# Second MLP: the first two products of units 0 to 2 moved ahead into the output projection's last token tiles

## The chip, the cores and the metric

One core of a Trainium2 chip runs the whole kernel as one launch. The metric is device time in microseconds (us) of that core; the figure to compare is the median over runs. PE is the matrix engine, VectorE (DVE in the profile), ScalarE (ACT) and GpSimd (POOL) are the elementwise engines, and SyncE (SP) issues the transfers. Each engine works through its own instructions strictly in the order in which the built program has them.

## The reference

A trunk of two layers over 1024 tokens of 1024 channels, all in fp32: layer 0 mixes by pooling, layer 1 by differential attention; each layer ends in a gated MLP with a convolution over three tokens.

```python
h = h + _diff_attention(_rms_norm(h, mix_norm[1]), ...)          # ends in o @ w_o, the output projection
h = h + _conv_ffn(_rms_norm(h, ffn_norm[1]), w_up[1], conv_w[1], conv_b[1], w_down[1])

def _conv_ffn(x, w_up, conv_w, conv_b, w_down):
    g, u = jnp.split(x @ w_up, 2, axis=-1)          # w_up is 1024 x 5632
    gc = conv_b + (three taps of g along the tokens)
    return (gelu(gc) * u) @ w_down                  # 2816 hidden channels
```

The change is about the seam between the two lines: the end of `o @ w_o` of layer 1, and the up half (`x @ w_up`) of the MLP behind it.

## The kernel before

**Up half of the MLP.** The 2816 hidden channels are 22 units of 128. For a unit, gate and up products are made together by a scheme of seven block products instead of eight: `product(j, i, acc, first)` is product i of unit j. Each is 12 matmuls of 128x512, four slices of the depth by three: fp32 operands are split in a high and a low part, and hi*hi, lo*hi and hi*lo are summed. The seven right operands `ar.x[i]` are shared by all units. `x[1]` and `x[2]` are the two depth halves of `hnT[0]`, so the normalized tokens of tiles 0 to 3 alone; `x[5]` and `x[3]` are `hnT[1]`, and `x[6]`, `x[7]`, `x[4]` are `xb` (the names x0, x1, x2 in the program): these five need tiles 4 to 7 as well. A unit's order is products 1, 6, 2, 7, 5, 4, 3. They accumulate in three PSUM tiles, `up_a` (1, 2), `up_b` (6, 7, 4) and `up_c` (5, 3).

**Weights.** `load(j)` issues two loads of 512 KB on SP into the `raw` pool (4 buffers, two units): the up half and then the gate half. `prep(j)` makes the seven left operands: four sums or differences of halves of them (`s_tile`, buffers from the `s` pool, 128x512), and for each product `parts`: ACT casts to `w_hi`, POOL subtracts to get `w_lo`, both into the `wc` pool (16 buffers, so eight products). For unit 0 VectorE does most of POOL's part. So POOL has 11 operations of 128x512 for each unit, four `s` and seven `w_lo`. When a unit's `s` and `w_lo` operations have read a `raw` buffer for the last time, SP may issue the load of the unit two further into it.

**The seam.** `wo_rest(tt)` does the output projection of one token tile, 24 matmuls `wo_acc` (L1251) from the 16 `wo_l` tiles that lie in `wc`; then residual and norm (`norm_to_x`): `xs` on ACT, eight transposes `tp` on PE (L299), and then, one tile later (`each_with_lag`), `combine` writes the operands of that tile (`put`: ACT the high part, VectorE or POOL the low part). Tiles 4 to 7 need the kept `xf` of tiles 0 to 3. The order of the tiles is `ORDER`. `next(mlp)` within it loads and prepares unit 0 early.

**What sets the order.** In the loop over units 1 to 21 the kernel text sets the order of PE, VectorE and ACT (`manual_schedule`); POOL and SP, and everything around the seam, are ordered by the scheduler at build time, which also respects how many buffers each pool has. The `s` pool has 4 buffers of 128x2x512, of which `s_tile` uses half of each.

```python
s1 = s_tile(g1, g2, ALU.add)           # g1, g2: gate half, u1, u2: up half of raw
s2 = s_tile(s1, u1, ALU.subtract)
w[6] = parts(s2, eng)
w[7] = parts(s_tile(u1, g1, ALU.subtract), eng)
w[5] = parts(s1, eng)
w[4] = parts(g2, eng)                  # the last read of the gate half
w[3] = parts(s_tile(u2, s2, ALU.subtract), eng)
```

Of the kernel before, what the change touches and what calls it, by code (L numbers as in the profile page):

```python
# [20 lines left out]
P = 128  # L21
# [68 lines left out]
def trunk_kernel(  # L90
# [133 lines left out]
    class Arena:  # L224


        def __init__(self, name):
            self.name = name
            self.s = None
# [57 lines left out]
    def norm_to_x(layer, tt, ar, h_t, ss):  # L287
        x, G = ar.x, nc.gpsimd
        r = rstd(ss)
        with tc.high_priority(offset=20 if layer else 0):  # L290
            xs = ar.tile("gc", [P, D], F32, "xs")
            A.mul(xs, h_t, r)
            nc.sync.dma_start(h_dram[3 * layer][tt], h_t)
            cs = slice((tt % 4) * P, (tt % 4 + 1) * P)
            pts = []
            for q in range(2):
                pt = ar.tile("ps_dn", [P, 4, P], F32, "tp")
                for k in range(4):
                    PE.transpose(pt[:, k], xs[:, (4 * q + k) * P:(4 * q + k + 1) * P], ident)  # L299
                pts.append(pt)  # L300

        def put(i, src, eng):
            hi, lo = x[i]
            A.copy(hi[:, :, cs], src)  # L304
            eng.tensor_tensor(lo[:, :, cs], src, f32(hi[:, :, cs]), ALU.subtract)  # L305

        def gained(q, dst):
            gk = gcol[:, 2 + layer, 4 * q:4 * q + 4].unsqueeze(2).broadcast_to([P, 4, P])
            V.tensor_tensor(dst, pts[q], gk, ALU.mult)
            return dst  # L310

        q0, q1 = slice(0, 4), slice(4, 8)
        if tt < 4:
            xf = ar.xf[tt] = ar.tile("raw", [P, NK, P], F32, "xf")
            gained(0, xf[:, q0])
            gained(1, xf[:, q1])

            def combine():
                with tc.high_priority(offset=50):
                    combine2()  # L320

            def combine2():
                put(1, xf[:, q0], (V if layer else G))
                put(2, xf[:, q1], G)
        else:
            xf = ar.xf.pop(tt - 4)
            b11, b21 = xf[:, q0], xf[:, q1]
            b12, b22 = (ar.tile("s", [P, 2, 512], F32, n)[:, 0].rearrange("p (k f) -> p k f", f=P) if layer else
                        ar.tile("wc", [P, 4, P], F32, n) for n in ("b12", "b22"))
            for k in range(4):  # L330
                A.mul(b12[:, k], pts[0][:, k], gcol[:, 2 + layer, k:k + 1])
            gained(1, b22)

            def combine():
                with tc.high_priority(offset=20 if layer else 0):
                    combine2()

            def combine2():
                t3 = ar.tile("u2", [P, 4, P], F32, "t3")
                V.tensor_tensor(t3, b22, b12, ALU.subtract)  # L340
                V.tensor_tensor(b12, b12, b11, ALU.subtract)
                V.tensor_tensor(b11, t3, b11, ALU.add)
                put(6, b11, V)
                V.tensor_tensor(b21, b21, b11, ALU.subtract)
                put(7, t3, G)
                put(5, b12, V)
                put(4, b21, G)
                put(3, b22, G)

        return combine  # L350

    def each_with_lag(tiles, first, early=None):
        late = None
        for tt in tiles:
            nxt = first(tt)
            if late is not None:
                late()
            late = nxt
            if tt == 1 and early is not None:
                early()  # L360
        late()

    def ffn(layer, ar, tail, extra=None):
# [4 lines left out]
        def load(j):  # L368
            if j >= NF:
                return  # L370
            raws.setdefault(j, [])
            for off in (DFF, 0):
                r = ar.tile("g" if layer == j == 0 else "raw", [P, NK, P], F32, "raw")
# [3 lines left out]
        def parts(src, eng=G):  # L377
            hi, lo = (ar.tile("wc", [P, 4, P], F32R, n) for n in ("w_hi", "w_lo"))
            A.copy(hi, src)  # L379
            eng.tensor_tensor(lo, src, f32(hi), ALU.subtract)  # L380
            return hi, lo

        def prep(j):
            if j >= NF:
                return
            w = ws.setdefault(j, {})
            ru, rg = raws.pop(j)
            u1, u2, g1, g2 = ru[:, 0:4], ru[:, 4:8], rg[:, 0:4], rg[:, 4:8]

            eng = (V, G)[j > 0]  # L390

            def s_tile(a, b, op):
                t = ar.tile("s", [P, 2, 512], F32, "s")[:, 0].rearrange("p (k f) -> p k f", f=P)
                eng.tensor_tensor(t, a, b, op)  # L394
                return t

            w[1] = parts(u1, G)
            if j == 0:
                w[2] = parts(u2, G)
# [5 lines left out]
            if j:  # L405
                w[2] = parts(u2)
            yield
            w[7] = parts(s_tile(u1, g1, ALU.subtract), eng)
            yield
            w[5] = parts(s1, eng)  # L410
            yield
            w[4] = parts(g2, eng)
            yield
            w[3] = parts(s_tile(u2, s2, ALU.subtract), eng)
            yield

        def product(j, i, acc, first):
            l, r = ws[j].pop(i), ar.x[i]
# [7 lines left out]
        def half(t, i):  # L426
            return t[:, 512 * i:512 * (i + 1)]
# [43 lines left out]
        def gated(j, g, gc, a, u2):  # L471
# [8 lines left out]
            else:  # L480
                for i, n in ((2, 1), (4, 0)):
                    nc.sync.dma_start(m_dram[i][c][:, qi], half(gc, n))
                comb.append(m_combos(j // 2, even.pop(), gc))

        def unit(j, nxt):
            def step():
                next(nxt, None)
# [5 lines left out]
                load_down(0)  # L493
                load_down(1)

            a = ar.tile("ps_up", [P, 512], F32, "up_a")
            product(j, 1, a, True)
            g = ar.tile("g", [P, S], F32, "g")
            A.copy(half(g, 0), a)  # L499
            if late:  # L500
                for _ in late.pop():
                    pass
# [9 lines left out]
            step()  # L512
            product(j, 2, a, False)
            next(side, None)
            step()
            product(j, 7, b, False)
            V.tensor_tensor(half(g, 1), b, half(g, 0), ALU.add)
            next(side, None)
            if last:
                for _ in prep_down(0):  # L520
                    pass
            step()
            c = ar.tile("ps_up", [P, 512], F32, "up_c")
            product(j, 5, c, True)
            V.tensor_tensor(half(g, 1), c, half(g, 1), ALU.add)
            next(side, None)
            if last:
                for _ in prep_down(1):
                    pass
            step()  # L530
            product(j, 4, b, False)
            V.tensor_tensor(half(g, 0), b, half(g, 0), ALU.add)
            step()
# [3 lines left out]
            product(j, 3, c, False)  # L537
            V.tensor_tensor(u2, c, u2, ALU.add)
# [170 lines left out]
            return ends[2:]  # L709

        load(0)
        first = prep(0)
        next(first)
        if layer:
            next(first)
        yield
        load(1)
        for _ in first:
            pass
        unit(0, prep(1))  # L720
        load(2)
        with tc.manual_schedule(engines=ENGINES):
            for j in range(1, NF):
                unit(j, prep(j + 1))
# [723 lines left out]
```

## Time and profile before

| | |
|---|---|
| runs | 2085.84, 2088.56, 2093.43 us; median 2088.56 |
| profiled execution | 2089.84 us, its span 2088.0 us |
| PE busy | 2003.6 us, 96% |
| DVE, ACT, POOL busy | 1560.6, 1024.4, 895.3 us |
| granted clock of PE | 0.983 on the mean |
| last `wo_acc` matmul starts | 1434.48 us |
| first matmul of the down half (`dn`) starts | 1870.23 us |

The span is the traced time of the program; what lies around it is 1.84 us. Shares are means over the whole program and say little of the seam, which is some 50 us long, and of the up half behind it, some 430 us. Two things of the profile have to be read with care: a matmul's shown duration (389 ns) is longer than the distance to the next one, since they are pipelined, and an engine that is busy for less than the whole time may still be the one that another waits for.

### The profile page before, as it was taken

The page shows a single profiled execution, that of the slowest core. Times are in us where ns is not written, and L with a number is a line of the kernel's source. Part 1 is how long each engine was busy: PE and PEld are TensorE (multiplying, and loading weights), DVE is VectorE, ACT ScalarE, POOL GpSimd, SP SyncE. Part 2 cuts the span into 40 slices and gives each one's busy share as a digit, 9 for nine tenths or more (in the row PEclk, how much of TensorE's full clock was granted, in tenths as well). Part 3 has the DMA queues.
Part 4 walks back from the last instruction along what each step waited for, and adds up shares of the span by engine and source line. Part 5 has one row for each costly group of instructions (what it writes and reads, how often), then busy time and mean ns, then how long its engine had stood idle before and what let it go on. Part 6 is the DMA issues. An engine that isn't in the chain of part 4 may idle for free.

```text
span 2088.0 us, 27647 instructions
## 1 busy us (share of the span) xinstructions
PE 2003.6 (96%) x9659; PEld 1665.6 (80%) x9659; DVE 1560.6 (75%) x2294; ACT 1024.4 (49%) x1838; POOL 895.3 (43%) x676
## 2 busy tenths in 40 slices
PE   5789999999999999999999998997999999999998
PEld 5768888888888877888888887875888888888886
DVE  6877777777665748899899888778667777775665
ACT  5743333333443645676667666456433333334443
POOL 4489999997000000101110110114999999930000
PEclk7889999999999999999999999999999999999999
DMA  4226445454876512122212115253345545458663
GB/s 153 99 70 198 141 154 184 132 177 151 334 239 221 207 56 66 48 75 61 61 46 77 54 35 197 101 172 118 121 160 167 172 149 179 142 191 334 201 211 132
DMA packets 221720, 301.90 MB, mean 145 GB/s; under 512 B 17852, under 2 KB 142092, under 8 KB 218764
## 3 DMA queue, kind: packets, MB, share of 16 engines
q1 hardware_dynamic: 221580, 300.13, 44.0%
q8 instruction: 76, 1.25, 0.2%
q14 instruction: 64, 0.52, 0.1%
HBM read 196.78 MB, written 90.70 MB: 138 GB/s over the span
## 4 chain that ended last, share of the span: by engine, by line
PE 59%; DVE 5%; ACT 2%; DMA 2%; issue 1%; SPq 1%; POOL 0%; ACTq 0%; DVEq 0%; POOLq 0%
PE dn L596 14%; PE up_b L422 8%; PE pj L1027 7%; PE up_c L422 5%; PE up_a L422 5%; PE sc L1113 5%; PE pj L1069 4%; PE po L1155 3%; PE aT L1144 3%; PE pj L1251 2%; DVE nm L1115 1%; DMA kf<-t 1%; ACT prob L1118 1%; DMA raw<-in_ffn_w_up_dram 0%; PE wo_acc L1251 0%
## 5 line engine op out<-in xcount | busy, mean ns | idle before, releaser
L1095 POOL TENSOR_TENSOR q_lo<-qt,q_hi 128x256 fp32r<-128x256 f32 x64 | 49.6, 776 | 683.4 <-ACT q_hi L1094 351.0
L380 POOL TENSOR_TENSOR w_lo<-s,w_hi 128x512 fp32r<-128x512 f32 x168 | 273.9, 1630 | 17.7 <-ACT w_hi L379 17.2
L596 PE MATMUL dn<-hnT_hi 128*128 128x512 f32 x560 | 218.3, 390 | 0.4 <-DVE hda L617 0.2
L596 PE MATMUL dn<-hnT_lo,hnT_hi 128*128 128x512 f32 x560 | 217.9, 389 | 0.0
L596 PE MATMUL dn<-hnT_hi,hnT_lo 128*128 128x512 f32 x560 | 217.9, 389 | 0.0
L422 PE MATMUL up_b<-x_hi,w_hi 128*128 128x512 f32 x528 | 207.2, 392 | 5.8 <-ACT x_hi L304 4.6
L422 PE MATMUL up_b<-x_lo,w_hi 128*128 128x512 f32 x528 | 206.4, 391 | 2.3 <-DVE x_lo L305 2.3
L380 POOL TENSOR_TENSOR w_lo<-raw,w_hi 128x512 fp32r<-128x512 f32 x130 | 195.1, 1501 | 30.0 <-ACT w_hi L379 26.5
L422 PE MATMUL up_b<-x_hi,w_lo 128*128 128x512 f32 x528 | 206.2, 391 | 0.0
L379 ACT CAST w_hi<-s 128x512 fp32r<-128x512 f32 x176 | 108.4, 616 | 179.1 <-PE up_b L422 87.3
L1115 DVE TENSOR_REDUCE nm<-sc 128x1 f32<-128x1024 f32 x128 | 155.8, 1217 | 15.7 <-PE sc L1113 15.0
L579 ACT CAST hnT_hi<-mst 128x1024 fp32r<-128x1024 f32 (+1 forms) x76 | 74.7, 983 | 164.7 <-PE dn L596 123.1
L1118 ACT ACTIVATE prob<-sc,nm 128x1024 f32<-128x1024 f32 x128 | 142.7, 1115 | 23.3 <-DVE nm L1115 11.6
L580 DVE TENSOR_TENSOR hnT_lo<-mst,hnT_hi 128x1024 fp32r<-128x1024 f32 (+1 forms) x76 | 86.5, 1138 | 90.1 <-ACT hnT_hi L579 90.1
L422 PE MATMUL up_a<-hnT_hi,w_hi 128*128 128x512 f32 x352 | 139.3, 396 | 1.4 <-ACT g L499 0.9
L422 PE MATMUL up_a<-hnT_lo,w_hi 128*128 128x512 f32 x352 | 138.8, 394 | 0.1
L422 PE MATMUL up_a<-hnT_hi,w_lo 128*128 128x512 f32 x352 | 138.5, 394 | 0.0
L394 POOL TENSOR_TENSOR s<-raw 128x512 f32<-128x512 f32 x84 | 133.1, 1584 | 10.3 <-DMA raw<-in_ffn_w_up_dram 4.1
L422 PE MATMUL up_c<-hnT_hi,w_lo 128*128 128x512 f32 x352 | 137.1, 389 | 0.3 <-DVE w_lo L380 0.3
L422 PE MATMUL up_c<-hnT_hi,w_hi 128*128 128x512 f32 x352 | 136.9, 389 | 0.0
L422 PE MATMUL up_c<-hnT_lo,w_hi 128*128 128x512 f32 x352 | 136.9, 389 | 0.0
L596 PEld LDWEIGHTS dn<-hnT_hi 128*128 128x128 f32 x560 | 105.1, 188 | 22.9 <-DVE hda L617 1.2
(304 smaller groups left out, 5433.3 us busy)
## 6 DMA issues: line engine op xcount, KB each, us to landing
raw<-in_ffn_w_up_dram SPq DMA_DIRECT2D x88, 512.0 KB, 4.3
mst<-m_dram SPq DMA_DIRECT2D x70, 512.0 KB, 6.2
wd<-in_ffn_w_down_dram SPq DMA_DIRECT2D x22, 1024.0 KB, 6.0
wd_dram<-wd SPq DMA_DIRECT2D x22, 1024.0 KB, 6.4
m_dram<-cm SPq DMA_DIRECT2D x80, 256.0 KB, 5.6
wst<-wd_dram SPq DMA_DIRECT2D x40, 512.0 KB, 4.8
m_dram<-gc SPq DMA_DIRECT2D x66, 256.0 KB, 6.3
wst<-in_ffn_w_down_dram SPq DMA_DIRECT2D x30, 512.0 KB, 7.2
```

Of the source, the lines that this page charges most:

```text
L379: A.copy(hi, src)
L380: eng.tensor_tensor(lo, src, f32(hi), ALU.subtract)
L394: eng.tensor_tensor(t, a, b, op)
L422: PE.matmul(acc, l[a][:, k], r[b][:, k], start=first and n == 0, stop=n == 11, skip_group_check=True)
L579: A.copy(h_, x)
L580: V.tensor_tensor(l_, x, f32(h_), ALU.subtract)
L596: PE.matmul(banks[t], l[:, q, cols], r[:, q], start=first and cnt == 0, stop=stop and cnt == 3 * n - 1, skip_group_check=True)
L1027: PE.matmul(acc, l[:, k % 2, h], r[:, k], start=(n == 0), stop=(n == 3 * NK - 1))
L1069: PE.matmul(acc, l[:, k % 4], r[:, k], start=(n == 0), stop=(n == 3 * NK - 1))
L1113: PE.matmul(sc[:, ns_], l[:, c], ks[:, c, ns_], start=(l is qhi), stop=(l is qlo))
L1115: V.tensor_reduce(nm, sc, AX.X, ALU.max, negate=True)
L1118: A.activation(soft[j, i][c], sc, AF.Exp, bias=nm, accum_out=sm[:, c, i:i + 1])
```

## The change

- `ORDER` goes from 0 4 1 5 2 6 3 7 to 0 4 1 5 2 3 6 7.
- For units 0 to 2 of layer 1 (`EARLY = {1: 3}`), products 1 and 2 are emitted (`start`) right behind the output projection's loop, ahead of the rest of unit 0; the scheduler places them. They need tiles 0 to 3 alone. These units then do products 6, 5, 7, 3, 4. The other 19 units and layer 0 keep their order.
- The weights come earlier: hooks after the first, third, fifth and eighth tile load unit 0, load unit 1 (into the buffers `wd` and `cm`, which are free then), and prepare products 1 and 2 of unit 0 and 1 of unit 1; the high and low parts of unit 0's two products go into the `s` pool.
- The `s` pool gets 9 buffers of 128x1x512 in place of 4 of 128x2x512 (4.5 instead of 4 of the old ones).
- In `combine2`, product 5's operand is written before product 7's, and 3's before 4's.

```diff
-ORDER = (0, 4, 1, 5, 2, 6, 3, 7)
+EARLY = {1: 3}
+ORDER = (0, 4, 1, 5, 2, 3, 6, 7)
...
-                self.s = pool(self.es_s, "s", bufs=4, side="right")
+                self.s = pool(self.es_s, "s", bufs=9, side="right")
+                self.s_shape = [P, 1, 512]
...
-                put(7, t3, G)
                 put(5, b12, V)
+                put(7, t3, G)
+                put(3, b22, G)
                 put(4, b21, G)
-                put(3, b22, G)
...
+            both = None
+            if layer in EARLY and j < 2:
+                both = ar.tile(("wd", "cm")[j], ((P, 2, D), (P, 4, 512))[j], F32, "raw2")
...
+            soon = j == 0 or 0 < j < EARLY.get(layer, 0)
+            where = "s" if layer == 1 and layer in EARLY and j == 0 else "wc"
+            w[1] = parts(u1, G, where)
+            if soon:
+                w[2] = parts(u2, G, where)
...
+            for i in (5, 7, 3, 4) if j < EARLY.get(layer, 0) else (7, 5, 4, 3):
+                w[i] = parts(rest[i](), eng)
+                yield
...
+        def start(j, i):
+            if i == 1:
+                a = ar.tile("ps_up", [P, 512], F32, "up_a")
+                product(j, 1, a, True)
+                g = ar.tile("g", [P, S], F32, "g")
+                A.copy(half(g, 0), a)
+                pre[j, 1] = a, g
+            else:
+                product(j, 2, pre[j, 1][0], False)
+                pre[j, 2] = True
...
+        if layer in EARLY:
+            yield
+            load(1)
+            yield
+            next(first)
+            yield
+            next(preps[1])
+            yield
+            load(2)
+            next(preps[2])
+            for j in range(EARLY[layer]):
+                for i in (1, 2):
+                    start(j, i)
...
-    each_with_lag(ORDER, wo_rest, lambda: next(mlp))
+    each_with_lag(ORDER, wo_rest, {0: lambda: next(mlp), 2: lambda: next(mlp),
+                                   4: lambda: next(mlp), 7: lambda: next(mlp)})
```

How the instructions stand: the counts of every engine stay as they were. Rows give line, operation, what is written and read (with buffer numbers), shape, and how many stand in a row.

PE at the end of the output projection, before. `wo_acc` is the projection's sum, `tp` a tile's transposes, `up_a_14135` product 1 of unit 0; the rows from the last `wo_acc` on:

```order
L1251 MATMUL wo_acc_14030<-wo_l_13502,hnT_lo1_70 128x512
L299 MATMUL tp_13999<-ident_66,xs_13996 128x128 x4
L299 MATMUL tp_14004<-ident_66,xs_13996 128x128 x4
L422 MATMUL up_a_14135<-hnT_hi0_67,w_hi_13721 128x512
L422 MATMUL up_a_14135<-hnT_lo0_68,w_hi_13721 128x512
```

After, from the last `wo_acc` on (`up_a_14125` is unit 0's product 1):

```order
L1306 MATMUL wo_acc_14013<-wo_l_13502,hnT_lo1_70 128x512
L428 MATMUL up_a_14125<-hnT_hi0_67,w_hi_13868 128x512
L428 MATMUL up_a_14125<-hnT_lo0_68,w_hi_13868 128x512
L428 MATMUL up_a_14125<-hnT_hi0_67,w_lo_13869 128x512
```

Behind it, the same engine's only transposes after the last `wo_acc`, those of tile 7, with the rows around them:

```order
L428 MATMUL up_a_14125<-hnT_hi0_67,w_hi_13872 128x512
L301 MATMUL tp_14058<-ident_66,xs_14055 128x128 x4
L301 MATMUL tp_14063<-ident_66,xs_14055 128x128 x4
L428 MATMUL up_a_14125<-hnT_lo0_68,w_hi_13872 128x512
```

So after the last `wo_acc`, before, PE has the transposes of tile 3 first and those of tile 7 ten matmuls later; after, 27 up matmuls stand first, then the transposes of tile 7, then the other 45 matmuls of the six moved products.

POOL in the middle of the up half, before; `w_lo_14699<-raw_14577` is unit 4's product 4, the last read of that `raw` buffer, into which SP loads the gate half of unit 6, `raw_14880`:

```order
L380 TENSOR_TENSOR w_lo_14699<-raw_14577,w_hi_14698 128x512
L380 TENSOR_TENSOR w_lo_14722<-s_14719,w_hi_14721 128x512
L394 TENSOR_TENSOR s_14872<-raw_14725,s_14773 128x512
L380 TENSOR_TENSOR w_lo_14750<-raw_14725,w_hi_14749 128x512
L380 TENSOR_TENSOR w_lo_14776<-s_14773,w_hi_14775 128x512
L394 TENSOR_TENSOR s_14923<-raw_14880 128x512
```

After, the same place (`raw_14575` is unit 4's gate half, `raw_14878` unit 6's, in the same buffer):

```order
L387 TENSOR_TENSOR w_lo_14697<-raw_14575,w_hi_14696 128x512
L401 TENSOR_TENSOR s_14921<-raw_14878 128x512
L401 TENSOR_TENSOR s_14923<-s_14921,raw_14876 128x512
L401 TENSOR_TENSOR s_14960<-raw_14876,raw_14878 128x512
L387 TENSOR_TENSOR w_lo_14720<-s_14717,w_hi_14719 128x512
L401 TENSOR_TENSOR s_15020<-raw_14876,s_14923 128x512
```

Before, four operations stand between the last read of the buffer and the first use of what is loaded into it; after, none. The same holds for the loads of units 4 to 21, which is 18 places.

More of the change, by code (lines that the diff above doesn't have):

```diff
@@ L327, in norm_to_x @@
             b11, b21 = xf[:, q0], xf[:, q1]
[L328 removed]
+            b12, b22 = (ar.tile("s", ar.s_shape, F32, n)[:, 0].rearrange("p (k f) -> p k f", f=P) if layer else
                         ar.tile("wc", [P, 4, P], F32, n) for n in ("b12", "b22"))
@@ L344, in combine2, with each_with_lag @@
                 V.tensor_tensor(b21, b21, b11, ALU.subtract)
+                put(5, b12, V)
                 put(7, t3, G)
-                put(5, b12, V)
+                put(3, b22, G)
                 put(4, b21, G)
-                put(3, b22, G)
         return combine
-    def each_with_lag(tiles, first, early=None):
+    def each_with_lag(tiles, first, hooks={}):
         late = None
-        for tt in tiles:
+        for k, tt in enumerate(tiles):
             nxt = first(tt)
@@ L358, in each_with_lag @@
             late = nxt
-            if tt == 1 and early is not None:
-                early()
+            if k in hooks:
+                hooks[k]()
         late()
@@ L371, in load, with parts @@
             raws.setdefault(j, [])
+            both = None
+            if layer in EARLY and j < 2:
+                both = ar.tile(("wd", "cm")[j], ((P, 2, D), (P, 4, 512))[j], F32, "raw2")
+                both = both.rearrange("p a b -> p (a b)").rearrange("p (e k f) -> p e k f", e=2, f=P)
             for off in (DFF, 0):
-                r = ar.tile("g" if layer == j == 0 else "raw", [P, NK, P], F32, "raw")
+                r = (ar.tile("g" if layer == j == 0 else "raw", [P, NK, P], F32, "raw") if both is None else
+                     both[:, 0 if off else 1])
                 nc.sync.dma_start(r, wup[:, off + j * P:off + (j + 1) * P].rearrange("(k p) f -> p k f", p=P))
                 raws[j].append(r)
-        def parts(src, eng=G):
-            hi, lo = (ar.tile("wc", [P, 4, P], F32R, n) for n in ("w_hi", "w_lo"))
+        def parts(src, eng=G, where="wc"):
+            hi, lo = (ar.tile(where, [P, 4, P], F32R, n) for n in ("w_hi", "w_lo"))
             A.copy(hi, src)
@@ L494, in unit @@
                 load_down(1)
[L496 to L499, printed above, removed]
+            if (j, 1) not in pre:
+                start(j, 1)
+            a, g = pre[j, 1]
             if late:
@@ L511, in unit @@
             next(side, None)
[L512 to L533, printed above, removed]
+            early = (j, 2) in pre
+            if early:
+                step()
+                c = ar.tile("ps_up", [P, 512], F32, "up_c")
+                product(j, 5, c, True)
+                V.tensor_tensor(half(g, 1), c, half(g, 0), ALU.add)
+                next(side, None)
+                step()
+                product(j, 7, b, False)
+                V.tensor_tensor(half(g, 1), b, half(g, 1), ALU.add)
+                next(side, None)
+                step()
+                product(j, 3, c, False)
+                V.tensor_tensor(u2, c, u2, ALU.add)
+                next(side, None)
+                step()
+                product(j, 4, b, False)
+                V.tensor_tensor(half(g, 0), b, half(g, 0), ALU.add)
+                step()
+            else:
+                step()
+                start(j, 2)
+                next(side, None)
+                step()
+                product(j, 7, b, False)
+                V.tensor_tensor(half(g, 1), b, half(g, 0), ALU.add)
+                next(side, None)
+                if last:
+                    for _ in prep_down(0):
+                        pass
+                step()
+                c = ar.tile("ps_up", [P, 512], F32, "up_c")
+                product(j, 5, c, True)
+                V.tensor_tensor(half(g, 1), c, half(g, 1), ALU.add)
+                next(side, None)
+                if last:
+                    for _ in prep_down(1):
+                        pass
+                step()
+                product(j, 4, b, False)
+                V.tensor_tensor(half(g, 0), b, half(g, 0), ALU.add)
+                step()
@@ L711, in ffn @@
         load(0)
-        first = prep(0)
-        next(first)
-        if layer:
-            next(first)
-        yield
-        load(1)
+        preps = [prep(j) for j in range(4)]
+        first = preps[0]
+        if layer in EARLY:
+            yield
+            load(1)
+            yield
+            next(first)
+            yield
[6 more added lines that the diff above has]
+                    start(j, i)
+        else:
+            next(first)
+            if layer:
+                next(first)
+            yield
+            load(1)
         for _ in first:
             pass
-        unit(0, prep(1))
-        load(2)
+        unit(0, preps[1])
+        if layer not in EARLY:
+            load(2)
         with tc.manual_schedule(engines=ENGINES):
             for j in range(1, NF):
-                unit(j, prep(j + 1))
+                unit(j, preps[j + 1] if j < 3 else prep(j + 1))
                 load(j + 2)
```

25 lines of the change are left out of this document (9 added, 16 removed).

## The prediction

> **What bounds the kernel now.** I read the page's busy times first, then a table by stage around the seam, then the waits, then the rows of PE and POOL, since the order of POOL is what moves most.
>
> ```profile
> PE 2003.6 (96%) x9659; PEld 1665.6 (80%) x9659; DVE 1560.6 (75%) x2294; ACT 1024.4 (49%) x1838; POOL 895.3 (43%) x676
> ```
>
> PE is the bound on the mean. By stage (time and length, then PE, weight loads, DVE, ACT, POOL busy and counts, PE's granted clock, share and rate of the transfers):
>
> ```profile
> 1435.00:1440.00 5.00, 0.36 (x2) 0.36 (x3) 5.00 (x7) 3.11 (x5) 3.39 (x2) 0.77 0.00 0
> 1440.00:1445.00 5.00, 4.34 (x14) 3.06 (x13) 4.33 (x11) 3.02 (x9) 2.55 (x2) 0.50 0.39 106
> 1450.00:1455.00 5.00, 3.38 (x13) 2.14 (x13) 4.86 (x6) 2.82 (x6) 3.28 (x2) 1.00 0.00 0
> 1480.00:1640.00 160.00, 160.00 (x708) 132.48 (x707) 111.54 (x110) 55.61 (x83) 157.18 (x99) 1.00 0.49 160
> 1700.00:1840.00 140.00, 140.00 (x619) 115.94 (x618) 107.05 (x97) 50.26 (x75) 127.45 (x81) 1.00 0.47 150
> ```
>
> Two things are to be seen. At the seam PE is nearly idle for 5 us and then runs at a granted clock of 0.50. In the up half, 1480 to 1640, PE is never idle, but POOL is busy for 157.18 of 160 us, 98%: it just keeps up. The wait at the seam and its end:
>
> ```profile
> PE tp L299 <- ACT xs L292: 9.8, 4, 4.8
> ```
>
> ```profile
> 1434.48 0.39 PE L1251 MATMUL wo_acc<-wo_l,hnT_lo 128*128 128x512 f32 x1
> 1439.64 1.97 PE L299 MATMUL tp<-ident,xs 128*128 128x128 f32 x8 [4.77 <-ACT xs L292]
> 1447.07 1.46 PE L299 MATMUL tp<-ident,xs 128*128 128x128 f32 x8
> 1870.23 0.39 PE L596 MATMUL dn<-hnT_hi 128*128 128x512 f32 x1
> ```
>
> From the last `wo_acc` (1434.48 + 0.39 = 1434.87) to the first `dn` are 435.4 us. In the chain of waits one product is this piece:
>
> ```profile
> 1481.44 2.72 PE up_c L422 x12
> ```
>
> So a product is 2.72 us, a unit of seven 19.04 us, and 22 units 418.9. The seam costs 435.4 - 418.9 = 16.5 us beyond the matmuls, 3.4 of them transposes, partly at the slow clock. That bounds what filling it can bring.
>
> **The change, part by part.**
>
> *The fill.* 72 matmuls (16.3 us) of units 0 to 2 now stand behind the last `wo_acc`, 27 of them (6.1 us) ahead of tile 7's transposes. Tile 7's `xs` sets when these can go:
>
> ```profile
> 1444.78 1.15 ACT L292 ACTIVATE xs<-hs,rs_r 128x1024 f32<-128x1024 f32 x1 [1.59 <-DVE rs_r L198]
> ```
>
> ```profile
> 1439.53 1.28 DVE L175 TENSOR_TENSOR hs<-wo_acc,hs 128x512 f32<-128x512 f32 x2
> ```
>
> Before, the residual add began 4.7 us after the last `wo_acc`, because VectorE was finishing tile 6, and `xs` was ready 6.4 us after it began (1445.9). After, tile 6 again precedes tile 7 on VectorE, so `xs` of tile 7 comes between 1441.3 (no backlog) and 1445.9; I take 1443.5. PE gets there at 1441.0, waits 2.5 us (0.3 to 4.9) instead of 4.77 and the following gaps, and 45 more matmuls cover the next step, tile 7's operands: before, the last of them on POOL,
>
> ```profile
> 1455.56 1.63 POOL L305 TENSOR_TENSOR x_lo<-xf,x_hi 128x512 fp32r<-128x512 f32 x1 [1.88 <-ACT x_hi L304]
> ```
>
> ended at 1457.2, 8.7 us after tile 7's transposes (1447.07 + 1.46). After: 1443.5 + 1.1 + 8.7 = 1453.3; I take 1452, between 1449 and 1455. If nothing else happened, PE would end the up half 16.5 - 2.5 - some 2 of transposes = 12 us sooner (8 to 14). The reorder of tiles 3 and 6 and of the four `put` is inside this figure; moved alone they would be worth what tile 6's operands then wait, 0 to 2 us either way, and I take 0. The earlier loads of units 0 and 1 are issued behind nothing that they wait for and land long before use; I take 0; if that cover, the projection's later tiles, were gone, the bound is the longest wait of the seam, 4.8 us. On SP they take the place of the first `wd` load, which moves behind unit 0's preparation on VectorE:
>
> ```profile
> wd<-in_ffn_w_down_dram SPq DMA_DIRECT2D x22, 1024.0 KB, 6.0
> ```
>
> VectorE combines it beside unit 1, which starts over 10 us after that; I take 0, and 6.0 us if it were issued only when needed.
>
> *POOL's order.* A unit is 11 POOL operations. Their durations, by group, between 1461 and 1640 (count, busy us, mean ns, idle before):
>
> ```profile
> L380 POOL TENSOR_TENSOR w_lo<-s,w_hi 128x512 fp32r<-128x512 f32 x39 | 65.5, 1679 | 0.0
> L380 POOL TENSOR_TENSOR w_lo<-raw,w_hi 128x512 fp32r<-128x512 f32 x29 | 47.3, 1632 | 0.0
> L394 POOL TENSOR_TENSOR s<-raw 128x512 f32<-128x512 f32 x22 | 34.4, 1566 | 5.6 <-DMA raw<-in_ffn_w_up_dram 4.1
> L394 POOL TENSOR_TENSOR s<-s,raw 128x512 f32<-128x512 f32 x11 | 17.2, 1561 | 0.8
> L394 POOL TENSOR_TENSOR s<-raw,s 128x512 f32<-128x512 f32 x10 | 14.9, 1494 | 0.7
> ```
>
> That is 179.3 us for 111. By the two stages above it is 157.18 / 99 = 1.588 and 127.45 / 81 = 1.573 each: 17.3 to 17.5 us for a unit, of PE's 19.04. What is left over is 1.6 us. What changes is where POOL's first `s` of a unit stands: before, four operations (6.3 us) after the last read of the `raw` buffer that its load refills; after, right behind that read, at 18 places. Then the load cannot be issued earlier than POOL needs it, and POOL stands still from issue to landing. The trace has this once, at unit 1, where the buffer was freed late:
>
> ```profile
> 1457.22 3.93 DMA raw<-in_ffn_w_up_dram
> 1461.31 0.10 POOL s L394
> ```
>
> ```profile
> POOL s L394 <- DMA raw<-in_ffn_w_up_dram: 4.1, 1, 4.1
> ```
>
> and all the loads of the up half took this long from issue to landing:
>
> ```profile
> DMA to landing us min/median/max: 3.7/4.3/8.6
> ```
>
> So a stall is 4.1 us by the one row, 3.7 to 8.6 by the others; I take 4.2. A page of the Trainium skill, "DMA: Bandwidth & Descriptors", section "Anatomy of one DMA", puts a transfer at about 2.0 us plus its bytes over 436 GB/s (fitted on another issue path), by estimate 3.2 us for 512 KB; the sum below would be 18 us lower by it. The rows are longer, and they decide.
>
> A POOL operation alone took 1.29 us, beside VectorE's long ones up to 2.27:
>
> ```profile
> 1461.31 1.29 POOL L394 TENSOR_TENSOR s<-raw 128x512 f32<-128x512 f32 x1 [4.12 <-DMA raw<-in_ffn_w_up_dram]
> 1489.55 2.27 POOL L380 TENSOR_TENSOR w_lo<-s,w_hi 128x512 fp32r<-128x512 f32 x1
> ```
>
> So 11 of them cost 14.2 us alone, and 3.1 to 3.3 us of a unit are collisions with VectorE. In a longer period the same VectorE work falls in part into the stall: 4.2 of some 21.4 us, a fifth, would take off 0.6. I take 17.2 us for the 11, only 0.1 to 0.3 under the rows, since VectorE's longest pair follows PE's product 4 and so comes when POOL has just started again. Bounds: 14.2, and 18.2 (1.65 each, between the two costliest groups).
>
> The new period is then 17.2 + 4.2 = 21.4 us, over PE's 19.04: POOL becomes the bound, and PE waits for `w_lo` of product 3, the first behind the stall, 2.4 us in every unit. PE's clock, I take it, stays full, as it did at a wait of 2.68 us, in a stage with a clock of 1.00:
>
> ```profile
> 1428.76 1.10 PE L299 MATMUL tp<-ident,xs 128*128 128x128 f32 x8 [2.68 <-ACT xs L292]
> ```
>
> ```profile
> 1420.00:1435.00 15.00, 12.19 (x58) 9.58 (x56) 12.89 (x25) 9.69 (x23) 5.63 (x5) 1.00 0.30 106
> ```
>
> At the seam, behind 4.77 us, nine matmuls took
>
> ```profile
> 1443.08 4.19 PE up_a L422 x9
> ```
>
> or 0.47 us each instead of 0.227. In each unit that would be 2.2 us more, 33 in all; I count it as outside the range.
>
> *The sum.* POOL begins the `s` of unit 1 at 1452, with no load to wait for (before: 1461.31). To the end of `w_lo` of unit 4's product 3 it has 47 operations, at 1.58, and three stalls: 1452 + 74.3 + 12.6 = 1538.9. From there to unit 19's product 3 are 15 periods, 321.0 us: 1859.9. The last load lies behind, so the last 15 products go at PE's pace, 40.8 us: 1900.7, against 1870.23 before. The up half ends 30.5 us later; the down half behind it starts as before and is unchanged. Against the profiled execution's 2089.84 that makes 2120.3 us; the median of the runs lies 1.28 lower, so 2119.
>
> VectorE and ACT follow PE in their fixed order and wait with it; neither is near its limit at 70% and 35% of the up half. Behind POOL's stalled operation stand the other 10 of its unit, and behind those PE alone; SP's next loads come 4 us later with it.
>
> **The rivals.**
>
> *The fill is kept.* The stall would be hidden if POOL ran several operations ahead of PE: eight products fit into `wc`, 21.8 us. For it: the filler starts POOL on unit 1 some 9 us sooner. Against it: PE is also sooner, and 18 stalls of 4.2 are 76 us against slack of 1.6 for each of 18 units, 29. It needs an excess of nothing, 11 operations and a stall in 19.04, so 1.35 us each or a landing of 1.7. Then the result is 2088.56 - 12 = 2077.
>
> *Collisions go away.* If all of VectorE's work that collides fell into the stalls, POOL's period would be 14.2 + 4.2 = 18.4 us, below 19.04, and the time that of the first rival, 2077; if half did, 1.45 us each, the period is 20.15, and the sum goes to 1452 + 68.2 + 12.6 + 302.3 + 40.8 = 1875.9, 5.7 us late: 2094. The Trainium skill, "SBUF — State Buffer", section "Who interferes with whom", has a rule that would do this: a VectorE instruction with two inputs in SBUF and a GpSimd one that reads SBUF exclude each other for the whole instruction, so time that POOL stands still is time in which VectorE blocks nobody. The trace agrees with it as far as the 1.29 and 2.27 go. But no order makes VectorE do this work just then, and it is spread over the unit (111.54 of 160 us busy).
>
> *Worse.* If each load takes as long as the slower ones, the stall is 5 us and operations stay at 1.62, the period is 22.8: 1452 + 76.1 + 15 + 342.3 + 40.8 = 1926.2, 56 us late: 2145. It is the far end of the likeliest case.
>
> *The filler doesn't fill.* If the wait for `xs` moves to 1445.9 and tile 7's operands follow 8.7 us later, POOL starts at 1455.7, and the sum is 4 us worse: 2123, or, without stalls, 2081. Both lie inside the other cases.
>
> **How the numbers follow.** Less than 0.5%, 10.4 us, cannot be told from no change. POOL bound by its stalls at 1.50 to 1.65 us each: 0.75, with 2119 and a range of its own from 2100 to 2142. Half of the collisions gone: 0.11, 2082 to 2100, counted as the same up to 2099. All hidden: 0.14, 2074 to 2080, most of it faster. So faster 0.12, same 0.13, slower 0.75. The range, 2077 to 2143, leaves out half of the lowest case and the ends of the likeliest, under 2 in 10.
>
> **What would show it.** In the profile after: POOL waits for DMA at L401, about 18 times some 4 us, 70 to 80 us in all; PE waits for POOL's `w_lo` in `up_c` about 16 times, 30 to 45 us; POOL's rows in the up half show an idle of 4 us behind each product 4; the seam shows PE nearly full from 1435 to 1455 with its clock at 1.00, and unit 3's first product earlier than before by some 5 to 10 us. I am wrong if POOL's waits for loads are few or short (then the build's order does not give the time), if they are there but PE does not wait (then POOL was ahead), or if the seam's wait only moves on.

## The result and the profile after

The changed kernel takes 2134.42 us in the median (2132.09 to 2140.32), against 2087.2 us for the kernel before, run beside it: a ratio of 1.0235, 95% interval 1.0215 to 1.0255. That is 47 us slower; 2119 was forecast, in a range from 2077 to 2143. The profiled execution has a span of 2134.4 us, 46.4 more than before. All of it lies between the last `wo_acc`, which starts 0.9 us earlier than before (1433.54), and the first `dn`, which starts at 1916.61 instead of 1870.23, also 46.4 later. The last `dn` follows 209.2 us behind the first in both.

The page's busy times, and the table by stage, with the same columns as in the table for the kernel before:

```profile
PE 2020.2 (95%) x9659; PEld 1670.6 (78%) x9659; DVE 1534.0 (72%) x2294; ACT 1024.1 (48%) x1838; POOL 880.4 (41%) x676
```

```profile
1435.00:1440.00 5.00, 3.59 (x16) 2.56 (x14) 4.96 (x7) 2.70 (x7) 4.20 (x3) 1.00 0.26 105
1440.00:1445.00 5.00, 3.99 (x14) 3.10 (x15) 2.61 (x6) 2.15 (x4) 1.73 (x1) 0.66 0.29 81
1480.00:1640.00 160.00, 147.12 (x622) 119.50 (x623) 99.50 (x105) 53.49 (x79) 122.85 (x80) 0.96 0.41 135
1700.00:1840.00 140.00, 127.69 (x532) 101.94 (x531) 77.84 (x82) 43.32 (x65) 107.90 (x73) 0.96 0.41 134
```

The seam is filled in part: from 1435 to 1440 PE is busy for 3.59 us instead of 0.36, at full clock, and from 1435 to 1455 for 17.0 us instead of 12.2. But from 1440 to 1445 its clock is 0.66. And in the up half PE is now idle for 12 to 13 us in each of the two long stages, and POOL, 98% busy before in the first of them, has fallen to 77% in both. It has the same operations to do; it waits. POOL's waits from 1440 to 1920, and PE's from 1376 to 1920:

```profile
POOL s L401 <- DMA raw<-in_ffn_w_up_dram: 90.0, 18, 6.1
POOL w_lo L387 <- ACT w_hi L386: 5.5, 4, 2.8
```

```profile
PE up_c L428 <- POOL w_lo L387: 21.3, 13, 2.5
PE up_b L428 <- DVE u L528: 13.2, 4, 6.8
PE tp L301 <- ACT xs L294: 8.0, 4, 3.1
PE up_a L428 <- POOL w_lo L387: 4.0, 9, 0.5
PE up_a L428 <- ACT g L498: 2.4, 1, 2.4
```

The last row is PE's wait at the seam. Product 2 of unit 0 adds into the same PSUM tile as product 1 and may do so only when ACT has copied product 1 out (`g`, at 1440.38); that copy stood in ACT's order behind casts that waited for VectorE. The seven matmuls behind this wait are the ones at the lower clock.

Before, POOL waited once for a load; now 18 times, 90.0 us in all. One of them in POOL's own rows, unit 4's last read of its gate half and the first `s` behind it, and SP's row between (start, duration):

```profile
1533.12 1.28 POOL L387 TENSOR_TENSOR w_lo<-raw,w_hi 128x512 fp32r<-128x512 f32 x1
1538.98 1.29 POOL L401 TENSOR_TENSOR s<-raw 128x512 f32<-128x512 f32 x1 [4.58 <-DMA raw<-in_ffn_w_up_dram]
```

```profile
1534.43 0.38 SPq L381 DMA_DIRECT2D raw<-in_ffn_w_up_dram  x1
```

The load is issued 0.03 us after the read ends, and POOL has nothing else to do until it lands. Later, the chain of waits runs through it, from POOL to the load and back to POOL, and then to PE's product 3:

```profile
1720.59 9.95 POOL w_lo L387 x6
1730.54 0.02 issue
1730.56 5.53 DMA raw<-in_ffn_w_up_dram
...
1740.40 1.27 POOL w_lo L387
1741.67 0.04 issue
1741.72 4.08 PE up_c L428 x10
```

PE's rows, from the last `wo_acc` to the first `dn`, added up by the wait that is named at the row behind a gap (matmuls at 0.2267 us; "slow" are larger distances without a named wait, most of them at a pitch of 0.43 us):

| us | before | changed | e1 | e2 | e3 | e4 | e5 | e9 | e10 |
|---|---|---|---|---|---|---|---|---|---|
| last `wo_acc` to first `dn` | 435.8 | 483.1 | 488.8 | 444.5 | 445.2 | 433.7 | 443.5 | 443.7 | 435.5 |
| 1848 up matmuls | 418.9 | 418.9 | 418.9 | 418.9 | 418.9 | 418.9 | 418.9 | 418.9 | 418.9 |
| wait for POOL `w_lo` | 0 | 29.0 | 38.5 | 0 | 0 | 0 | 0 | 0 | 0 |
| wait for DVE `u`, `g` | 0.4 | 13.8 | 0.4 | 10.4 | 10.8 | 0.5 | 9.8 | 3.1 | 1.3 |
| wait for ACT `xs`, `x_hi`, `g` | 6.7 | 2.6 | 8.4 | 5.4 | 2.7 | 9.6 | 5.5 | 15.8 | 6.9 |
| slow | 3.5 | 15.7 | 16.3 | 7.3 | 10.0 | 2.5 | 7.0 | 3.6 | 4.1 |

The rest are transposes and smaller waits. The columns e1 to e10 are experiments of the next section.

### The profile page after: what moved, and what is told of

Read it like the earlier page. It is cut to its first block, busy times and chain, and to the rows that moved or that the text cites. A ratio compares the mean times of both kernels' runs of the same rounds, so it can differ in the third digit from the quotient of the medians.

```text
span 2134.4 us, 27704 instructions
## 1 busy us (share of the span) xinstructions
PE 2020.2 (95%) x9659; PEld 1670.6 (78%) x9659; DVE 1534.0 (72%) x2294; ACT 1024.1 (48%) x1838; POOL 880.4 (41%) x676
## 4 chain that ended last, share of the span: by engine, by line
PE 76%; DVE 8%; POOL 6%; DMA 4%; ACT 3%; issue 2%; SPq 1%; POOLq 0%; ACTq 0%; DVEq 0%
PE dn L635 18%; PE up_b L428 13%; PE up_c L428 9%; PE up_a L428 8%; PE pj L1082 7%; PE sc L1168 5%; POOL w_lo L387 5%; PE pj L1124 4%; PE po L1210 3%; PE aT L1199 2%; DMA raw<-in_ffn_w_up_dram 2%; PE pj L1306 2%; POOL s L401 2%; PE wo_acc L1306 1%; PE pp L903 1%
## 5 line engine op out<-in xcount | busy, mean ns | idle before, releaser
L387 POOL TENSOR_TENSOR w_lo<-s,w_hi 128x512 fp32r<-128x512 f32 x168 | 265.1, 1583 | 12.3 <-ACT w_hi L386 12.0
L1170 DVE TENSOR_REDUCE nm<-sc 128x1 f32<-128x1024 f32 x128 | 155.7, 1217 | 16.3 <-PE sc L1168 15.5
L428 PEld LDWEIGHTS up_b<-x_hi,w_hi 128*128 128x128 f32 x528 | 100.6, 190 | 42.6 <-ACT w_hi L386 12.2
```

The source lines that it names most:

```text
L428: PE.matmul(acc, l[a][:, k], r[b][:, k], start=first and n == 0, stop=n == 11, skip_group_check=True)
L1170: V.tensor_reduce(nm, sc, AX.X, ALU.max, negate=True)
```

## The experiments

Theory A: the deeper `s` pool lets the scheduler put a unit's first `s` right behind the read that frees the buffer of its load; POOL then needs 17 + 5 us for a unit and sets the pace. Theory B, the rival that the profile after suggests: the early units, whose product 7 waits up to 6.8 us for VectorE's `u`, and the slow clock behind these waits. Theory C: the order of the tiles.

**e1: the kernel before, with the deeper pool alone.**

```diff
...
-                self.s = pool(self.es_s, "s", bufs=4, side="right")
+                self.s = pool(self.es_s, "s", bufs=9, side="right")
+                self.s_shape = [P, 1, 512]
...
```

The two places that take a buffer of the pool use `s_shape` in place of `[P, 2, 512]`.

> The kernel before, with nothing of the change but the s pool: 9 buffers of 128x1x512 in place of 4 of 128x2x512. In the built order POOL's first s of a unit then stands right behind the last read of the raw buffer at 18 places, as in the changed kernel; no product is moved. Theory A (POOL's order: each of these 18 loads is waited for by 5 us, and POOL with 17 + 5 us a unit sets the pace): POOL starts unit 1 at 1461 as before, some 6 us later than in the changed kernel, then 22.0 us a unit: 45 to 55 us slower than before, POOL waits for DMA about 90 us in all. Theory B (the early units' product 7 waiting for VectorE's u, 13 us, and the slow clock behind these waits cost the time; POOL's waits are beside it): no change, 2085 to 2091, since no unit is early here. Theory C (the order of tiles 3 and 6): no change.

2137.25 us, ratio 1.0245 (1.0217 to 1.0272). The number and size of the pool's buffers alone, with no product moved, cost as much as the whole change. Its POOL waits:

```profile
POOL s L395 <- DMA raw<-in_ffn_w_up_dram: 98.0, 20, 6.7
```

Theory A had 45 to 55 us; 51 came. B and C, which had no change here, fall as causes of the total.

**e2: the changed kernel, `s_tile` in a pool of its own.**

```diff
-                self.s = pool(self.es_s, "s", bufs=9, side="right")
+                self.s = pool(self.es_s, "s", bufs=5, side="right")
+                self.s4 = pool(self.es_s, "s4", bufs=4, side="right")
                 self.s_shape = [P, 1, 512]
...
-                t = ar.tile("s", ar.s_shape, F32, "s")[:, 0].rearrange("p (k f) -> p k f", f=P)
+                t = ar.tile("s4" if layer else "s", ar.s_shape, F32, "s")[:, 0].rearrange("p (k f) -> p k f", f=P)
```

> The changed kernel with s_tile in a pool of its own of 4 buffers of 128x1x512 and 5 buffers for the rest: the same memory, but in the built order four POOL operations again stand between the last read of a raw buffer and the first use of its refill. All else of the change stays. Theory A: POOL's 18 waits go, PE sets the pace; what is left is the early units' wait for VectorE (13.2 us, with some 4.5 us of slow clock) against the fill: region 418.9 + 1.1 + 16.7 + 6.8 = 443.5 us from 1433.8, so 1877, 7 us later than before: 2094, between 2088 and 2100. Theory B: most of the loss stays, 2115 to 2135. Theory C: stays at 2134.

2099.11 us, ratio 1.0059 (1.0043 to 1.0075), at the upper end of what A had. The same memory in another division takes 35 us off the changed kernel. POOL waits for no load any more, and its most frequent wait is now for ACT's `w_hi`, which mostly waits for PE: POOL is ahead.

```profile
POOL w_lo L388 <- ACT w_hi L387: 46.8, 38, 11.6
```

**e3: the changed kernel, POOL in the text's order.**

```diff
-        with tc.manual_schedule(engines=ENGINES):
+        with tc.manual_schedule(engines=ENGINES | ({mybir.EngineType.Pool} if layer else set())):
             for j in range(1, NF):
```

> The changed kernel with POOL added to the engines whose order the kernel text sets in the up loop of layer 1: the s pool stays at 9 buffers, but POOL does a unit's operations where the text has them, and a refill is issued more than 30 operations before its use. Theory A: as with the split pool, 2094, between 2086 and 2102; it shows that order and not the number of buffers decides. Theory B: 2115 to 2135. Theory C: 2134.

2099.07 us, ratio 1.0062 (1.0044 to 1.0080), with the pool still at 9 buffers. POOL waits for no load here either. So it is the order that costs; the depth only allowed it.

**e4: the kernel before, the tile order alone.** `ORDER = (0, 4, 1, 5, 2, 3, 6, 7)`.

> The kernel before with the tile order 0 4 1 5 2 3 6 7 alone. Theories A and B: within 3 us of before, 2084 to 2092. Theory C (the order of the tiles costs the time): above 2110.

2087.67 us, ratio 1.0010 (0.9998 to 1.0022): nothing, as A and B had it. In its trace PE's wait for `xs` goes from 4.8 to 0.9 us, and the one for tile 7's operands (`x_hi`) from 0.6 to 5.8.

With POOL's order mended, e2 and e3 are still 12 to 13 us slower than before, where the prediction had put the fill at 12 us faster. In e2's profile 8.7 us of it lie between the last `wo_acc` and the first `dn` (444.5 against 435.8). PE's largest gaps there, in units 0 to 2:

```profile
PE up_b L429 <- DVE u L529: 9.9, 3, 4.8
```

In the changed kernel VectorE's rows at the longest of these waits (start, duration, line):

```profile
1473.96 2.42 DVE L574 SCALAR_TENSOR_TENSOR gc<-g,convp,gc 128x1023 f32<-128x1023 f32 x1 [1.31 <-ACT gc L573]
1476.41 2.20 DVE L578 SCALAR_TENSOR_TENSOR gc<-g,convp,gc 128x1023 f32<-128x1023 f32 x1
1481.08 0.69 DVE L480 TENSOR_TENSOR gc<-up_a,gc 128x512 f32<-128x512 f32 x1 [2.46 <-ACT gc L479]
1481.69 1.76 DVE L481 TENSOR_TENSOR gc<-u,gc 128x512 f32<-128x512 f32 x1
1483.37 0.68 DVE L528 TENSOR_TENSOR u<-up_b,g 128x512 f32<-128x512 f32 x1
```

```profile
1484.19 0.77 PE L428 MATMUL up_b<-x_hi,w_hi 128*128 128x512 f32 x1 [6.84 <-DVE u L528]
```

L574 to L481 are the convolution and gating of unit 0, in VectorE's fixed order ahead of unit 1's `u` (L528), which must read `up_b` before product 7 may add to it. ACT is a part of this chain: VectorE itself waits 2.46 us for ACT's `gc`. In a usual unit product 1 stands ahead of product 6 and product 2 behind it, 5.4 us of PE's work during which VectorE can finish; the early units have given these two away and have only product 5.

**e5: e2, and in the early units that tail behind `u` instead of ahead of it.** (`late` holds the unfinished tail of the unit before; `tail_of_last` finishes it, with the lines that stood at the place of the old loop.)

```diff
-            if late:
-                for _ in late.pop():
-                    pass
...
+            if not early:
+                tail_of_last()
             step()
             b = ar.tile("ps_up", [P, 512], F32, "up_b")
             product(j, 6, b, True)
             u2 = ar.tile("u2", [P, 512], F32, "u2")
             V.tensor_tensor(u2, b, half(g, 0), ALU.add)
+            if early:
+                tail_of_last()
```

> The kernel of e2 (s_tile's pool split off), and in the early units the tail of the unit before (the gated products, VectorE's work of several us) is emitted behind VectorE's u of product 6 instead of ahead of it. In e2's profile PE waits 10.4 us for this u, and 7.3 us go to slow matmuls, most of them behind these waits. Theory A (two separate causes, POOL's order and this wait): both go, about 15 us less than e2: 2084, between 2078 and 2090, so the fill brings 2 to 8 us against before and not the 12 of the prediction. Theory D (VectorE is what limits the early units, whatever its order): the wait moves to the next VectorE result, 2094 to 2100.

2101.18 us, ratio 1.0071 (1.0057 to 1.0085): no gain, and 1 us above the range of theory D (VectorE limits the early units in any order). The wait moved on, as D had it, to VectorE's next result, product 5's, which product 3 needs:

```profile
1490.25 0.77 PE L429 MATMUL up_c<-hnT_hi,w_hi 128*128 128x512 f32 x1 [4.22 <-DVE g L544]
```

**e6: e3 with the same move.**

> The kernel of e3 (POOL in the text's order), with the same move of the tail behind u in the early units. Theory A: as the split pool with it, 2084, between 2078 and 2090. Theory D: 2094 to 2100.

2099.56 us, ratio 1.0056 (1.0039 to 1.0073): no gain over e3, again as D.

**e7: the changed kernel with the same move.**

> The changed kernel with this move alone; POOL's order stays as it is, with 18 waits for loads. Theory A: POOL sets the pace at 22 us a unit, and what PE gains in units 1 and 2 it waits for later; only what POOL itself lost there (3.5 us of waiting for w_hi) comes back: 2134 minus 0 to 5, so 2129 to 2134. Theory B (VectorE's wait in the early units is a cost of its own that adds to POOL's): 13.8 us and its slow clock come off, 2116 to 2120.

2138.86 us, ratio 1.0250 (1.0236 to 1.0264), not below the changed kernel's 2134.42, nor in the range of A or B. The move takes 6.2 us off VectorE's wait (7.6 us are left of 13.8 in PE's gaps), and PE's wait for `w_lo` grows from 29.0 to 32.7 us: part of what VectorE gives back POOL takes, as A had it. In the profiles the stretch from the last `wo_acc` to the first `dn` is 3.7 us shorter than in the changed kernel (479.4 against 483.1), within A's 0 to 5, but the last `wo_acc` starts 5.2 us later (1438.76). So in these two profiles the longer time comes from ahead of the seam; why stays open. The last `wo_acc` starts anywhere from 1426.1 to 1438.8 in the profiles of this document.

**e8: the changed kernel, two of a unit's `w_lo` on VectorE.**

```diff
-                w[2] = parts(u2)
+                w[2] = parts(u2, V if layer else G)
...
-                w[i] = parts(rest[i](), eng)
+                w[i] = parts(rest[i](), V if layer and i == 5 else eng)
```

> The changed kernel with two of a unit's seven w_lo (products 2 and 5, all units but the first) on VectorE instead of POOL. In the built order the refill of a raw buffer is still waited for at the same places, with one operation between instead of none, so POOL's waits stay, some 3.4 us each, 55 to 65 in all. Theory A (a matter of rate: 11 operations and a wait exceed PE's 19.04 us): 9 operations at 1.6 and 3.4 are 17.8, POOL no longer sets the pace, PE's waits for w_lo go: 2099 as with the split pool, between 2094 and 2106. Theory E (a matter of latency: each wait of POOL holds up PE by itself): 18 times 1 to 2 us of waiting stay, 2115 to 2134.

2105.88 us, ratio 1.0093 (1.0077 to 1.0109), at the end of A's range and well under E's. PE doesn't wait for `w_lo` at all. The expected 55 to 65 us of POOL's waits for loads were wrong:

```profile
POOL w_lo L387 <- ACT w_hi L386: 74.4, 22, 6.8
POOL s L401 <- DMA raw<-in_ffn_w_up_dram: 12.3, 9, 4.1
```

With 9 operations POOL is ahead of PE and stands at the one `w_lo` that is now between the freed buffer and the `s`, waiting for `w_hi` and through it for PE, while the load lands. With enough slack the tight order costs PE no wait for `w_lo`; it is a matter of rate. PE's waits for VectorE's `u` are 14.1 us here, against 10.4 in e2.

**e9: e2 with `EARLY = {1: 1}`**, so the two products of unit 0 alone are moved.

> The kernel of e2 (s_tile's pool split off) with EARLY = {1: 1}: the products 1 and 2 of unit 0 alone are moved, so units 1 and 2 do theirs in place and the tail of the unit before has 8 us of PE's work in front of it again. Theory A with D (in the early units VectorE's chain of results sets the pace, since these units have 13.6 us of PE's work instead of 19.04): the waits for VectorE's u go, but 24 matmuls (5.4 us) no longer cover tile 7's chain of about 16 us from the last wo_acc: some 9 us of waiting there, 2 to 4 us of slow clock: 2084 to 2090, the time of before. If the waits of units 1 and 2 were not from the missing products: 2094 to 2100, as e2.

2094.48 us, ratio 1.0042 (1.0029 to 1.0055): slower than A with D had it, and by the number in the range of the other theory, that the waits of units 1 and 2 were not from the missing products. The waits decide against that one: those for `u` fall to 3.1 us from 10.4. What was taken too small is the seam, some 9 us of waiting; PE waits 11.28 us at once there:

```profile
1456.59 0.80 PE L429 MATMUL up_b<-x_hi,w_hi 128*128 128x512 f32 x1 [11.28 <-ACT x_hi L307]
```

**e10: e2 with `EARLY = {1: 2}`**, and in the early units the tail behind product 7's result.

> The kernel of e2 with EARLY = {1: 2}, and in the early units the tail of the unit before behind VectorE's result of product 7 (with three early units the PSUM buffers would not allow it). 48 matmuls (10.9 us) cover all but some 4 us of tile 7's chain, and unit 1 waits for no tail before its product 3. Theory D, in the form that it is the place of the tail in VectorE's order: 8 us less than before, 2079, between 2074 and 2085. Theory D in the form that VectorE has too much to do in these units in any order: the wait moves on once more, 2090 to 2100.

2090.08 us, ratio 1.0028 (1.0017 to 1.0038): by the number at the lower end of D's second form (2090 to 2100), but without the wait that this form had: those for `u` are gone (1.3 us), and no other of VectorE's results is waited for as long. The hoped-for 2079 isn't there. It is the best version that I have, 2.1% faster than the changed kernel, and no faster than the kernel before. The stage 1434 to 1456, before and in e10:

```profile
1434.00:1456.00 22.00, 13.61 (x47) 9.52 (x46) 17.52 (x31) 13.69 (x28) 9.69 (x7) 0.77 0.15 48
1434.00:1456.00 22.00, 14.97 (x55) 10.54 (x53) 21.62 (x24) 12.38 (x25) 17.95 (x12) 0.86 0.28 96
```

VectorE is busy for 21.62 of 22 us, PE for 14.97. At the seam VectorE has become the full engine, with the operands of tiles 6 and 7 and unit 0's weights. It has fewer instructions there than before, 24 instead of 31, and they are longer, 0.90 us instead of 0.57 in the mean, while POOL is busy for 17.95 us instead of 9.69. How much of that is POOL's working beside them and how much the other mix of instructions was not separated. That PE's work put there only moves the moment at which it waits is a reading of these rows and not shown. Whether a version with less of VectorE's work at the seam would win was not tried.

## Why the prediction was right, point by point

- **POOL's order, the stalls, POOL as the bound:** right. 18 waits for loads were named, and 18 came; e1 has the loss from this alone, and e2 and e3 lose it.
- **The sum was 16 us short** (30.5 forecast, 46.4 in the profiles), and the time lay in the range all the same. By its three terms: to the end of unit 4's product 3 on POOL 1538.9, measured 1545.1 (+6.2); the 15 periods 321.0, measured 329.4 to 1874.5, where PE's product 3 of unit 19 gets its `w_lo` (+8.4); the last 15 products 40.8, measured 42.1 (+1.3, the slow clock behind the last wait).
- **The mis-sized term is the stall:** 4.2 taken, 90.0 / 18 = 5.0 measured. The first three were as taken (13.0 us in all, against 12.6), the other 15 were 77.0 us, 5.1 each, which is 14 us more over the periods. I took the one wait in the trace, 4.1, near the bottom of the quoted 3.7 to 8.6. The 11 operations went the other way: 17.2 taken, 329.4 - 77.0 = 252.4 over 15 periods, 16.8, measured; the period was 22.0 instead of 21.4. So the two errors worked against each other.
- **POOL's start** of unit 1's `s`: 1452, measured 1455.41, past the end of the given 1449 to 1455, and where "the filler doesn't fill" had put it (1455.7). Tile 7's `xs` was ready at 1443.9, near the 1443.5 taken; from the end of its transposes (1445.35) to the end of its last operand on POOL (1455.45) it took 10.1 us where 8.7 was taken, and for the step from 1453.3 down to 1452 the prediction gave no row. The first term's other part is 4.2 us of POOL's waiting for `w_hi` (the 2.8 of the row above, 0.7 and 0.7), the longest because ACT's casts stood behind its `gc` (L479), which had waited 3.8 us for VectorE; POOL's 47 operations took 1.9 less than I had.
- **PE's waits for `w_lo`** were to be about 16, 30 to 45 us; they are 13 in the row for `up_c`, 29.0 us with the others in PE's gaps, and begin only at 1610, since PE was late itself before that.
- **"PE's clock stays full"** was wrong:

```profile
1655.00:1658.00 3.00, 2.56 (x12) 1.76 (x10) 1.43 (x3) 0.00 (x0) 3.00 (x3) 1.00 0.00 0
1742.00:1745.00 3.00, 3.00 (x8) 2.32 (x9) 0.75 (x1) 0.00 (x0) 3.00 (x2) 0.50 0.00 0
```

```profile
1654.55 0.50 PE L428 MATMUL up_c<-hnT_hi,w_lo 128*128 128x512 f32 x1 [2.44 <-POOL w_lo L387]
1741.72 0.79 PE L428 MATMUL up_c<-hnT_hi,w_lo 128*128 128x512 f32 x1 [2.23 <-POOL w_lo L387]
1786.20 0.80 PE L428 MATMUL up_c<-hnT_hi,w_lo 128*128 128x512 f32 x1 [2.54 <-POOL w_lo L387]
```

  Behind four of PE's six waits of 1.9 to 2.5 us for `w_lo` the matmuls are slow for a while, 0.43 us apart, at a granted clock of 0.50 in the one shown; behind the other two they are not (the one of 2.44 us is shown). The trace doesn't say what decides between them. 15.7 us were slow, against 3.5 before. As POOL sets the pace, little of it should reach the end, since PE would else have waited for POOL; that is argued and not measured.
- **The fill, 12 us sooner without stalls,** was wrong in sign. The step that failed is "if nothing else happened": taking products 1 and 2 out of units 0 to 2 takes away what covered VectorE's tail of the unit before. The prediction had VectorE waiting behind PE, and not PE behind VectorE ("VectorE and ACT follow PE in their fixed order and wait with it"). Unit 3's first product, forecast 5 to 10 us earlier than before, starts at 1515.27 instead of 1508.47. In the changed kernel most of this is hidden behind POOL's pace, which is why the forecast could do without it; in e2 it shows. There PE loses 25.6 us beyond the matmuls, against 16.9 before; 10.4 of them are waits for `u`, and some 4 are the 20 slow matmuls behind these. The rest is about 11, so by this estimate the seam itself gained 5 to 6 us, half of what was forecast. The 2.5 us that the prediction left at the seam came out in size (2.42) by luck: PE waits there for ACT's `g` and not for `xs`. So the two rivals that end at 2077 had a wrong time as well.
- **The rivals:** "the fill is kept" had POOL's stalls hidden from PE, and PE's 29.0 us of waiting for `w_lo` exclude it; "collisions go away" needed operations of 1.29 us, or 1.45 for its half, and they took 1.53. "Worse" had the stall right, at 5 us, and the operations too long, at 1.62. By the rule of the Trainium skill, "SBUF — State Buffer", "Who interferes with whom", a VectorE instruction with two inputs in SBUF and a GpSimd one that reads SBUF exclude each other, so operations of POOL would get shorter where VectorE works in its stalls. The trace agrees in sign (1.588 us each before in the stage from 1480, 16.8 / 11 = 1.53 over the 15 periods after), but it is 0.6 us of a unit's 3.1 to 3.3. The other estimate from the Trainium skill, "DMA: Bandwidth & Descriptors", "Anatomy of one DMA", 3.2 us a load by a fit on another issue path, is 1.8 under the measured wait of 5.0.

## What to carry to other kernels

A pool's depth is also a limit on how far the scheduler may move an operation ahead, and e1 lost 51 us by taking that limit away. After enlarging a pool, look in the built order for an operation that now stands directly behind the read that frees the buffer of its own load, and count the stall into that engine's period, against its slack. Work that is moved ahead as a filler also leaves a hole where it came from; ask what it covered there, on the engines behind PE. And look at the second engine of the stage to be filled: in e10 VectorE was busy for 98% of it, and filling PE gained nothing.

## What the runs showed of the hardware

POOL's wait for a 512 KB load into a buffer just freed was not one number. From 1626 on it alternated from unit to unit: 4.4 to 4.7 us in one, 5.4 to 6.1 in the next, the longer ones with three stores of 256 KB issued 1.5 to 3.8 us before the load, the shorter ones with none in that time. One of the longer:

```profile
1726.34 0.38 SPq L381 DMA_DIRECT2D raw<-in_ffn_w_up_dram  x1
1726.82 1.53 SPq L472 DMA_DIRECT2D m_dram<-cm  x3
1730.56 0.38 SPq L381 DMA_DIRECT2D raw<-in_ffn_w_up_dram  x1
```

The wait behind the last of these rows was 5.69 us. No run takes the stores away, so that they are the cause is not shown. The page's median from issue to landing, 4.3 us over the kernel's 88 such loads, hides the difference; a latency that an engine stands still for has to be read from rows with the same transfers beside it.
